# FFN gate and up projections as seven block products in two token passes

## The chip, the cores and the metric

The kernel runs on one core of a Trainium2 chip. What counts is device time in microseconds from one launch to its end, as the median of several runs. The engines are TensorE (PE; its weight loads PEld are listed apart), VectorE (DVE), ScalarE (ACT), GpSimd (POOL) and SyncE (SP), which here only issues DMAs. Each engine works through its own queue in order and waits on semaphores for the others.

## What is computed

One step of a two-layer backbone on 1280 tokens (1024 latent, then 256 context) of width 1024. Layer 0 mixes by neighbourhood attention and a state-space scan, layer 1 by a Fourier transform. Each layer ends with an FFN whose width D_FF is 2816 = 22 x 128. Cut to the FFN:

```python
def _swiglu(h, wg, wu, wd):
    return (jax.nn.silu(h @ wg) * (h @ wu)) @ wd
# in each layer, with shift, scale and gate from the conditioning:
# h = rmsnorm(x, g) * (1 + scale) + shift
# x = x + gate * _swiglu(h, w_gate, w_up, w_down)
```

## The kernel before

Activations lie channels on partitions, tokens along the free axis, as eight tiles xT[kt] of 128 x 1280 (the residual). Tokens go in three chunks, CH: 512, 512 and 256; the first two are latent, the third is context with its own conditioning. A product in full precision is made of three fp32r matmuls: each operand is split in a high part (a ScalarE cast) and a low part (a subtraction of the high part), and high x high, low x high and high x low are summed in PSUM (lines 104 to 111 and 99 to 102).

The function ffn (line 125) takes the 22 column blocks f of 128 one by one. G(f,c) is the gate product of chunk c, 8 x 3 matmuls of up to 512 columns, then SiLU on ScalarE; U(f,c) is the up product, after which VectorE multiplies (L142), ScalarE casts the high part (L143) and VectorE makes the low part (L144). DNp adds the down products of a pair of blocks to the residual, one PSUM bank for each output tile d and chunk, evacuated by one VectorE operation (L158). The loop alternates: gate and up of two blocks, then the 24 down sums of the pair before. Activations stay in SBUF. Weights come by SyncE DMA as 128 x 1024 tiles, wsplit (line 91) casts them on ScalarE (L95) and subtracts on GpSimd (L96).

In layer 0 the generator side = mods_v (line 922) runs beside the FFN: the conditioning vectors of layer 1, six of 1024. It loads w_mod in 128 x 512 pieces into two buffers, VectorE multiplies and adds each piece for the two conditionings (L901, L902), TensorE sums over partitions (L906). One piece is taken at each G and U. In layer 1 there is no side work.

Before the FFN the norm of each chunk is made: Rms sums squares as the residual's tiles are finished, rms_done turns them into 1/rms (TensorE sums L40, small VectorE operations, TensorE broadcast L55, a copy into R), modnorm (line 74) scales, shifts and splits into the operand tiles h. In layer 0 the attention's output projection first does chunk 0 for all d, then chunks 2 and 1; the first block's gate and up products of chunk 0 follow as soon as its norm is there. The Fourier output projection fnet_out (line 823) ends with the same sums.

The tile framework gives out buffers from pools: a tile waits until an earlier one with its tag is released. It orders each engine's instructions by the program's order where they are ready by its own estimate, so a stream may differ from the text in places.

Of the kernel before, what the change touches and what calls it, by code (L numbers as in the profile page):

```python
# [124 lines left out]
def ffn(k, wg, wu, wd, gate, h, order, side=iter(()), fin=lambda d,c: None, mid=lambda: None):  # L125
    """yields before it first reads h of a chunk, in the order given; mid(): called at points within the first block; fin(d,c): called when the residual's tile d is complete on chunk c; fin(KT,1) where its running sum is"""
    nc=k.nc; sh=[128,KT,128]
    at=k.at
    gs={}; us={}; ds={}; acts={}
    def sg(f):  # L130
        if f<NF: gs[f]=wsplit(k,wg[f],sh)
    def su(f):
        if f<NF: us[f]=wsplit(k,wu[f],sh)
    def sd(f):
        if f<NF: ds[f]=wsplit(k,wd[f].rearrange("p (k m) -> p k m",k=KT),sh,tag="dn",pool=k.dn)
    def G(f,c):
        p=proj(k,gs[f],h,c); s=at(CH[c][1])
        nc.scalar.activation(s,p,AF.Silu); return s  # L138
    def U(f,c,s,mid=lambda: None):
        p=proj(k,us[f],h,c,mid); n=CH[c][1]  # L140
        ah=at(n,F32R); al=at(n,F32R)
        nc.vector.tensor_tensor(out=s,in0=s,in1=p,op=ALU.mult)  # L142
        nc.scalar.copy(ah,s)  # L143
        nc.vector.tensor_tensor(out=al,in0=s,in1=ah,op=ALU.subtract)  # L144
        acts[f,c]=(ah,al)
# [8 lines left out]
    def DNp(fs,d,c):
        c0,n=CH[c]; p=bank(k)[:,:n]
        mm3(k,p,[(ds[f][i][:,d],acts[f,c][j]) for f in fs for i,j in ((0,0),(1,0),(0,1))])
        xs=k.xT[d][:,c0:c0+n]
        nc.vector.scalar_tensor_tensor(out=xs,in0=p,scalar=gate(d,c),in1=xs,op0=ALU.mult,op1=ALU.add)  # L158
    sg(0); su(0)
    for i,c in enumerate(order):  # L160
        yield
        g=G(0,c); mid()
        U(0,c,g,mid)
    sg(1); su(1); sd(0); sd(1); GU(1)
    for j in range(NF//2):
        fs=(2*j,2*j+1)
        if 2*j+2<NF:
            GU(2*j+2)
            for d in range(KT):
                for c in range(3): DNp(fs,d,c)  # L170
            sd(2*j+2); sd(2*j+3)
            GU(2*j+3,range(3) if 2*j+4<NF else range(2))
        else:
            for c in range(3):
# [1036 lines left out]
```

## Time and profile before

| | |
|---|---|
| three runs | 3035.39, 3030.21, 3035.36 us; median 3035.36 |
| profiled execution | span 3035.6 us, mean granted TensorE clock 0.965 |
| layer 0 | rest of the output projection and FFN: first product at 809.8, last down product at 1821.9 |
| layer 1 | FFN: first product at 2073.8, last down product at 3014.9 |

The profile is one execution. Its rows give busy times of engines, groups of instructions by line and tile, what an idle engine waited for, and the chain of work that ended last, followed back from the end. Matmul durations overlap: the pace is the distance from one start to the next, not the duration.

### The profile page before, as it was taken

Reading aid. Unit: us, or ns where it says so; the run is one execution under the profiler, and the core shown is the slowest. Engines: PE = TensorE matmul, PEld = TensorE weight load, DVE = VectorE, ACT = ScalarE, POOL = GpSimd, SP = SyncE. Lnnn points to the kernel's source line nnn. Section 1 sums busy time; section 2 is a strip of 40 time slices with the busy share of each in tenths; the row PEclk is TensorE's granted clock in tenths of the full one; section 3 lists DMA queues with packets and bytes.
Section 4 is the critical chain, followed back from the end, with each engine's and each line's share of the span. In section 5 each row is a group of like instructions: output and inputs, shape, how many; then the busy total and the mean of one; then the engine's idle time right before and its main releaser. Section 6 shows DMA issues by size and latency. Waiting matters only on the chain. (4 is left out here: it accounts for less than half of the span.)

```text
span 3035.6 us, 40128 instructions
## 1 busy us (share of the span) xinstructions
PE 2818.0 (93%) x15982; PEld 2338.7 (77%) x15982; DVE 1589.5 (52%) x2710; ACT 802.9 (26%) x1512; POOL 963.0 (32%) x709
## 2 busy tenths in 40 slices
PE   3778889888999999999999997998999999999997
PEld 1556667677788888888888886886888888888885
DVE  8788823888465445545554248276332223332335
ACT  3333344666342111111111123244111111111113
POOL 3666636454432111111111135264111111111114
PEclk7889999999999999999999998998999999999998
DMA  6244465354303222222212112421111111111101
GB/s 223 79 117 131 139 165 167 107 126 142 108 28 104 71 69 63 73 67 70 84 56 63 42 63 79 139 70 35 32 38 42 42 35 42 35 37 41 36 28 70
DMA packets 158563, 239.81 MB, mean 79 GB/s; under 512 B 22300, under 2 KB 97692, under 8 KB 158376
## 3 DMA queue, kind: packets, MB, share of 16 engines
q1 hardware_dynamic: 155784, 232.52, 25.2%
q0 software_dynamic: 2592, 4.73, 0.5%
q8 instruction: 125, 2.05, 0.3%
q14 instruction: 62, 0.51, 0.1%
HBM read 209.52 MB, written 27.69 MB: 78 GB/s over the span
## 5 line engine op out<-in xcount | busy, mean ns | idle before, releaser
L110 PE MATMUL p<-h,wh 128*128 128x512 f32 (+1 forms) x4480 | 1201.3, 356 | 10.4 <-DVE h L85 5.8
L110 PEld LDWEIGHTS p<-h,wh 128*128 128x128 f32 x4480 | 790.8, 189 | 145.4 <-DVE h L85 8.1
L96 POOL TENSOR_TENSOR wl<-raw,wh 128x1024 fp32r<-128x1024 f32 (+1 forms) x200 | 425.2, 2132 | 1498.6 <-ACT wh L95 1495.6
L110 PE MATMUL p<-h,wl 128*128 128x512 f32 (+1 forms) x2240 | 794.8, 355 | 0.5 <-POOL wl L96 0.5
L102 PE MATMUL p<-a,wh 128*128 128x512 f32 (+1 forms) x2112 | 572.9, 357 | 1.6 <-ACT a L143 1.6
L110 PEld LDWEIGHTS p<-h,wl 128*128 128x128 f32 x2240 | 423.5, 189 | 66.1 <-POOL wl L96 1.1
L142 DVE TENSOR_TENSOR a<-a,p 128x512 f32<-128x512 f32 x132 | 78.8, 597 | 681.4 <-PE p L110 681.4
L158 DVE SCALAR_TENSOR_TENSOR xt<-p,mod,xt 128x512 f32<-128x512 f32 (+1 forms) x528 | 336.2, 659 | 174.5 <-PE p L102 173.9
L102 PEld LDWEIGHTS p<-a,wh 128*128 128x128 f32 x2112 | 374.3, 188 | 67.3 <-ACT a L143 1.9
L102 PE MATMUL p<-a,wl 128*128 128x512 f32 (+1 forms) x1056 | 376.8, 357 | 0.0
L95 ACT CAST wh<-raw 128x1024 fp32r<-128x1024 f32 (+1 forms) x200 | 181.6, 919 | 688.3 <-PE p L102 370.9
L102 PEld LDWEIGHTS p<-a,wl 128*128 128x128 f32 x1056 | 198.6, 188 | 32.2 <-issue 0.5
L143 ACT CAST a<-a 128x512 fp32r<-128x512 f32 x132 | 72.3, 548 | 555.6 <-DVE a L142 411.1
L122 PE MATMUL p<-h,wh 128*128 128x512 f32 (+1 forms) x576 | 181.7, 385 | 19.4 <-ACT h L71 11.9
L144 DVE TENSOR_TENSOR a<-a 128x512 fp32r<-128x512 f32 (+1 forms) x132 | 146.0, 1107 | 65.2 <-ACT a L143 64.4
L138 ACT ACTIVATE a<-p 128x512 f32<-128x512 f32 x132 | 69.2, 524 | 373.0 <-PE p L110 360.9
L122 PEld LDWEIGHTS p<-h,wh 128*128 128x128 f32 x576 | 107.1, 196 | 51.6 <-ACT h L71 13.4
L902 DVE SCALAR_TENSOR_TENSOR ma<-mw,sc,ma 128x512 f32<-128x512 f32 x84 | 101.8, 1212 | 57.7 <-DMA mw<-in_w_mod_dram 57.2
L122 PE MATMUL p<-h,wl 128*128 128x512 f32 (+1 forms) x288 | 106.1, 369 | 0.0
L544 POOL TENSOR_TENSOR P<-P,l 128x384 f32<-128x384 f32 (+1 forms) x80 | 68.0, 852 | 105.7 <-DVE l L541 67.9
L550 ACT ACTIVATE P<-P,m 128x896 f32<-128x896 f32 x64 | 66.7, 1042 | 32.5 <-DVE m L549 32.3
L548 DVE CUSTOM_DVE_ANT_0 P<-S,bt 128x896 f32<-128x896 f32 x64 | 69.2, 1082 | 11.1 <-DMA bt<-T_dr 5.3
(372 smaller groups left out, 3526.3 us busy)
## 6 DMA issues: line engine op xcount, KB each, us to landing
mw<-in_w_mod_dram SPq DMA_DIRECT2D x160, 256.0 KB
raw<-in_wg_dram SPq DMA_DIRECT2D x44, 512.0 KB
raw<-in_wu_dram SPq DMA_DIRECT2D x44, 512.0 KB
raw<-in_wd_dram SPq DMA_DIRECT2D x44, 512.0 KB
xt<-in_x_dram SPq DMA_DIRECT2D x16, 640.0 KB
hf<-in_w_mod_dram SPq DMA_DIRECT2D x16, 512.0 KB
raw<-in_w_in_dram SPq DMA_DIRECT2D x24, 256.0 KB
raw<-q_dr SPq DMA_DIRECT2D x16, 320.0 KB
```

Source lines behind the costliest of these rows:

```text
L95: nc.scalar.copy(h,raw)
L96: nc.gpsimd.tensor_tensor(out=l,in0=raw,in1=h,op=ALU.subtract)
L102: k.nc.tensor.matmul(p,lhsT=w,rhs=x,start=i==0,stop=i==n-1)
L110: k.nc.tensor.matmul(p,lhsT=w[i][:,kt],rhs=h[c][j][:,kt],start=kt==0 and m==0,stop=kt==KT-1 and m==2)
L122: k.nc.tensor.matmul(ps[c],lhsT=w[i][:,kt],rhs=h[c][j][:,4*pc+kt],start=pc==0 and kt==0 and m==0,stop=pc==1 and kt==3 and m==2)
L138: nc.scalar.activation(s,p,AF.Silu); return s
L142: nc.vector.tensor_tensor(out=s,in0=s,in1=p,op=ALU.mult)
L143: nc.scalar.copy(ah,s)
L144: nc.vector.tensor_tensor(out=al,in0=s,in1=ah,op=ALU.subtract)
L158: nc.vector.scalar_tensor_tensor(out=xs,in0=p,scalar=gate(d,c),in1=xs,op0=ALU.mult,op1=ALU.add)
L548: V.tensor_tensor_reduce(out=P,in0=S,in1=b,op0=ALU.add,op1=ALU.max,scale=1.0,scalar=-3.0e38,accum_out=m)
L902: else: V.scalar_tensor_tensor(out=acc[s],in0=w,scalar=sc,in1=acc[s],op0=ALU.mult,op1=ALU.add)
```

## The change

The two projections of the FFN become block products after Strassen (Winograd's form). The 1024 input channels are halved (channel tiles 0 to 3 and 4 to 7), the 2816 columns are halved (block f goes with block f + 11), and a pass of 640 tokens is halved into 320 and 320. A 2 x 2 block product then takes seven products of 4 x 3 matmuls on 320 columns instead of eight. There are two passes over the tokens, 11 units each, 22 units in a layer, and 14 steps in a unit (STEP: gate or up X, product P). All of gate and up comes first; the activations go to DRAM (act) and come back for the down products, which are a second phase with the same matmuls as before.

Weight side: prep() makes the sums and differences of the four weight blocks on VectorE, wslot() splits each (cast on ScalarE, low part on GpSimd for products 1, 2, 4 and on VectorE for 6, 5, 7, 3); five steps are prepared ahead. Token side: early() makes the first two operands of the first pass in layer 0, full() the whole first pass, stage() the second pass's operands in units 3 to 6, which are parked in DRAM (hop), and fetch() brings them back and splits them in unit 10. Product side: step() gathers the products in three PSUM banks for each of gate and up, with ScalarE reading the first of each and VectorE adding; at the end VectorE multiplies gate by up. mods_v is now taken once after each step, in pieces of 128 x 256 (four quarters of eight loads and one closing piece for each vector). The down phase has one generator for its loads, casts and splits.

fnet_out takes its scratch from the new pool E and sums squares in two halves of 640 tokens. In layer 0 the norm of chunk 0 is finished and the old pool closed before the rest of the output projection. Comments and docstrings are gone everywhere. The core of the diff:

```diff
-def ffn(k, wg, wu, wd, gate, h, order, side=iter(()), fin=lambda d,c: None, mid=lambda: None):
...
-    def GU(f,cs=range(3)):
-        ss={}
-        for c in cs: ss[c]=G(f,c); next(side,None)
-        sg(f+1)
-        for c in cs:
-            U(f,c,ss[c])
-            next(side,None)
-        su(f+1)
-    def DNp(fs,d,c):
-        c0,n=CH[c]; p=bank(k)[:,:n]
-        mm3(k,p,[(ds[f][i][:,d],acts[f,c][j]) for f in fs for i,j in ((0,0),(1,0),(0,1))])
...
+PAIRS=NF//2; HALF=320
+STEP=((0,1),(1,1),(0,2),(1,2),(0,6),(1,6),(0,5),(0,7),(1,5),(1,7),(0,4),(0,3),(1,4),(1,3))
+SLOT={1:0,2:1,6:2,5:3,7:4,4:5,3:6}
...
+def wslot(k, src, eng):
+    w=k.E.tile([128,2,4,128],F32R,tag="w",bufs=7,name="w")
+    k.nc.scalar.copy(w[:,0],src); eng.tensor_tensor(out=w[:,1],in0=src,in1=w[:,0],op=ALU.subtract)
+    return w
+def rawt(k, src):
+    t=k.E.tile([128,8,128],F32,tag="raw",bufs=6,name="raw"); k.nc.sync.dma_start(t,src); return t
...
+    AHEAD=5
+        self.seq=[(u,X,P) for u in range(2*PAIRS) for X,P in STEP]
...
+    def early(self):
+        k=self.k; nc=k.nc; self.first=True
+        for kt in range(KT):
+            t=k.at(HALF); s=kt//4; self.scaled(t,kt,0,HALF)
+            hi=self.ops.hi(s)[:,kt%4]; self.shifted(hi,t,kt,0,HALF)
+            nc.vector.scalar_tensor_tensor(out=self.ops.lo(s)[:,kt%4],in0=t,scalar=self.S(kt,0),in1=hi,op0=ALU.add,op1=ALU.subtract)
...
+    def full(self):
+        k=self.k; V=k.nc.vector; G=k.nc.gpsimd; h=[]
+        def tt(o,i,j,op): V.tensor_tensor(out=o,in0=i,in1=j,op=op)
+        for kt in range(KT):
+            t=k.at(2*HALF); h.append(t); self.scaled(t,kt,0,2*HALF); self.shifted(t,t,kt,0,2*HALF)
+            if not self.first: self.split(kt//4,kt%4,t[:,0:HALF],G if kt%2 else V)
+        L=slice(0,HALF); N=slice(HALF,2*HALF)
+        for i in range(4):
+            a,b=h[i],h[i+4]
+            self.split(6,i,b[:,N],G)
+            tt(a[:,L],a[:,N],a[:,L],ALU.subtract)
+            tt(a[:,N],b[:,N],a[:,N],ALU.subtract)
+            tt(b[:,N],b[:,N],a[:,L],ALU.subtract)
+            self.split(2,i,b[:,N])
+        for i in range(4): self.split(3,i,h[i][:,L])
+        for i in range(4): self.split(4,i,h[i][:,N],G)
+        for i in range(4):
+            tt(h[i+4][:,L],h[i+4][:,L],h[i+4][:,N],ALU.subtract); self.split(5,i,h[i+4][:,L])
+    def stage(self, i):
+        k=self.k; nc=k.nc; V=nc.vector; t0=2*HALF; L=slice(0,HALF); N=slice(HALF,2*HALF)
+        def tt(o,x,y): V.tensor_tensor(out=o,in0=x,in1=y,op=ALU.subtract)
+        def put(s,t): nc.sync.dma_start(self.hop[s][:,HALF*i:HALF*i+HALF],t)
+        a,b,c,d=[k.at(2*HALF) for _ in range(4)]
+        for t,kt in ((a,i),(b,i+4)): self.scaled(t,kt,t0,2*HALF); self.shifted(t,t,kt,t0,2*HALF)
+        put(0,a[:,L]); put(1,b[:,L]); put(6,b[:,N])
+        tt(c[:,L],a[:,N],a[:,L]); tt(c[:,N],b[:,N],a[:,N]); put(3,c[:,L]); put(4,c[:,N])
+        tt(d[:,L],b[:,N],c[:,L]); tt(d[:,N],b[:,L],d[:,L]); put(2,d[:,L]); put(5,d[:,N])
+    def fetch(self, s):
+        nc=self.k.nc; hi,lo=self.ops.hi(s),self.ops.lo(s); r=lo.bitcast(F32)
+        nc.sync.dma_start(r,self.hop[s].rearrange("p (k n) -> p k n",k=4))
+        nc.scalar.copy(hi,r); (nc.gpsimd if s in (1,5) else nc.vector).tensor_tensor(out=lo,in0=r,in1=hi,op=ALU.subtract)
+    def load(self, u, half):
+        if u<2*PAIRS:
+            for X in range(2): self.raw[u,X,half]=rawt(self.k,self.w[X][u%PAIRS+PAIRS*half])
+    def prep(self):
+        if self.np==len(self.seq): return
+        i=self.np; self.np+=1; u,X,P=self.seq[i]; k=self.k; V=k.nc.vector
+        def tt(o,x,y,op=ALU.subtract): V.tensor_tensor(out=o,in0=x,in1=y,op=op)
+        r1=self.raw[u,X,0]; a11,a12=r1[:,0:4],r1[:,4:8]
+        if P not in (1,2): r2=self.raw[u,X,1]; a21,a22=r2[:,0:4],r2[:,4:8]
+        if P==6:
+            s3=self.st[X]=k.E.tile([128,4,128],F32,tag="st",bufs=2,name="st")
+            tt(s3,a11,a21); tt(a21,a21,a22,ALU.add); tt(a11,a21,a11)
+        if P==3: tt(a12,a12,a11)
+        src=a11 if P in (1,6) else a12 if P in (2,3) else a21 if P==5 else a22 if P==4 else self.st[X]
+        self.ws[i]=wslot(k,src,k.nc.gpsimd if P in (1,2,4) else V)
+    def start(self):
+        for _ in range(self.AHEAD): self.prep()
+    def step(self, i):
+        k=self.k; nc=k.nc; V=nc.vector; u,X,P=self.seq[i]; e=self.es
+        if P==1:
+            for b in "ABC": e[X,b]=bank(k)[:,0:HALF]
+            e[X,1]=k.at(2*HALF)
+        if P==7: e[X,2]=k.at(2*HALF)
+        p=e[X,"A" if P in (1,6,7,4) else "B" if P==2 else "C"]; w=self.ws.pop(i); x=(self.ops.hi(SLOT[P]),self.ops.lo(SLOT[P]))
+        n=0
+        for kt in range(4):
+            for a,b in ((0,0),(1,0),(0,1)):
+                nc.tensor.matmul(p,lhsT=w[:,a,kt],rhs=x[b][:,kt],start=P in (1,2,5) and n==0,stop=n==11,skip_group_check=P!=2); n+=1
+        L=slice(0,HALF); N=slice(HALF,2*HALF); e1,e2=e[X,1],e.get((X,2))
+        def done(o):
+            if X==0: nc.scalar.activation(o,o,AF.Silu)
+        def add(o): V.tensor_tensor(out=o,in0=p if P!=7 else e[X,"C"],in1=o,op=ALU.add); done(o)
+        def mul(b,s):
+            g=e[0,b][:,s]; V.tensor_tensor(out=g,in0=g,in1=e[1,b][:,s],op=ALU.mult)
+        if P==1: nc.scalar.copy(e1[:,L],p)
+        elif P==2: add(e1[:,L])
+        elif P==6: nc.scalar.copy(e1[:,N],p)
+        elif P==7: nc.scalar.copy(e2[:,N],p); add(e2[:,N])
+        elif P==4:
+            if X==0: nc.scalar.activation(e2[:,L],p,AF.Silu)
+            else:
+                g=e[0,2]; V.tensor_tensor(out=g[:,L],in0=g[:,L],in1=p,op=ALU.mult)
+                mul(2,N); self.out(u,1,g)
+        elif P==3:
+            add(e1[:,N])
+            if X==1: mul(1,L); mul(1,N); self.out(u,0,e[0,1])
+    def out(self, u, half, t):
+        p,f=divmod(u,PAIRS); self.k.nc.sync.dma_start(self.act[f+PAIRS*half][:,2*HALF*p:2*HALF*p+2*HALF],t)
+    def run(self, fin=lambda d,c: None):
+        last=PAIRS-1; self.dprep()
+        for i,(u,X,P) in enumerate(self.seq):
+            s=i%len(STEP)
+            if s==2: self.load(u+1,0)
+            if s==12: self.load(u+1,1)
+            self.prep(); self.step(i); next(self.side,None)
+            if u in (3,4,5,6) and s==5: self.stage(u-3)
+            if u==last and X==1: self.fetch(SLOT[P])
+            if u==2*PAIRS-1 and s in (6,9,11,13): next(self.dn)
+        for _ in self.side: pass
+        self.down(fin)
...
+            for j in range(PAIRS):
+                fs=(2*j,2*j+1); raws=[rawt(k,self.wd[f].rearrange("p (k m) -> p k m",k=KT)) for f in fs]
+                for i,f in enumerate(fs):
+                    t=k.H.tile([128,3840],F32,tag=f"h{f%4}",name="ac"); self.ac[f]=t
+                    nc.sync.dma_start(t[:,0:NT],self.act[f])
+                yield
+                for i,f in enumerate(fs):
+                    t=self.ac[f]; hi=t[:,NT:2*NT].bitcast(F32R); lo=t[:,2*NT:3*NT].bitcast(F32R)
+                    nc.scalar.copy(hi,t[:,0:NT]); (nc.gpsimd if i else nc.vector).tensor_tensor(out=lo,in0=t[:,0:NT],in1=hi,op=ALU.subtract)
+                    self.ac[f]=(hi,lo)
+                yield
+                for dh in range(2):
+                    for i,f in enumerate(fs): self.ds[f,dh]=wslot(k,raws[i][:,4*dh:4*dh+4],nc.gpsimd)
+                    yield
+        self.dn=gen()
...
+        for j in range(PAIRS-1):
+                if d in (0,2,4,6): next(self.dn,None)
+                for c in range(3): one((2*j,2*j+1),d,c)
+        for c in range(3):
+            if c==2: fin(KT,1)
+            for d in range(KT): one((NF-2,NF-1),d,c); fin(d,c)
...
+def mods_v(k, us):
+    a,b=k.at(512),k.at(512); n=[0]
+    def mw(): n[0]+=1; return a[:,256*(n[0]%2):256*(n[0]%2)+256]
+    for u in us: yield from mod_unit_v(k,u,mw,[b[:,256*i:256*i+256] for i in range(2)])
...
+    act=dr("act",[NF,128,NT]); hop=dr("hop",[7,128,4*HALF])
...
+        wout(d,0,p); r0.add(d)
+    r0.done(Rt[0])
+    arp.__exit__(None,None,None); Ep=epool()
...
+    F=FFN(k,*ffw(0),mv(0,5),mv(0,4),mv(0,3),Rall,act,hop)
...
+        if d==2: F.early()
...
+    F.load(0,0); F.load(0,1); F.start()
+    r[1].done(Rt[1]); r[2].done(Rt[2])
+    F.full(); F.side=mods_v(k,[(1,j) for j in range(6)])
+    F.run(fin)
...
+    F=FFN(k,*ffw(1),mv(1,5),mv(1,4),mv(1,3),Rall,act,hop)
+    r=fnet_out(k,io,mv(1,2),*AB,lambda: (F.load(0,0),F.load(0,1)))
+    F.start()
+    F.full(); F.run(fin2)
```

The helpers that it calls: scaled() is one VectorE operation (residual times scale times R) on each stretch of latent or context tokens, shifted() one ScalarE operation that adds the shift, split() a ScalarE cast and a subtraction on the engine given, Ops the table of the 14 operand pieces in the six tiles that held h. In mod_unit_v the loop runs over quarters of 256 columns instead of halves of 512.

## Rows read from the trace of the kernel before

**Rows 1.** The page: span, then busy us (share of the span) xinstructions.

```profile
span 3035.6 us, 40128 instructions
...
PE 2818.0 (93%) x15982; PEld 2338.7 (77%) x15982; DVE 1589.5 (52%) x2710; ACT 802.9 (26%) x1512; POOL 963.0 (32%) x709
```

**Rows 2.** Stretches: length, busy us of PE, PEld, DVE, ACT, POOL; clock, DMA, GB/s.

```profile
973.00:1640.00 667.00, 667.00 (x3520) 563.08 (x3519) 335.22 (x471) 100.66 (x154) 116.48 (x48) 1.00 0.24 72
...
2060.00:2115.00 55.00, 43.80 (x186) 33.39 (x187) 42.23 (x73) 28.84 (x52) 24.61 (x17) 0.84 0.04 10
...
2250.00:2950.00 700.00, 700.00 (x3615) 592.10 (x3614) 229.42 (x314) 99.80 (x148) 117.14 (x49) 1.00 0.12 37
```

**Rows 3.** Chain in order of time, layer 1's FFN: start, us, what.

```profile
2111.62 56.12 PE p L110 x287
2167.74 27.85 PE p L102 x144
2195.59 56.08 PE p L110 x288
...
2531.36 55.69 PE p L110 x288
```

**Rows 4.** Timeline of PE in the Fourier output projection.

```profile
1998.78 1.63 PE L845 MATMUL O<-h,wpm 128*128 128x320 f32 x10
...
2002.85 2.06 PE L840 MATMUL E<-h,wpm 128*128 128x322 f32 x12
...
2005.57 3.78 PE L845 MATMUL O<-h,wpm 128*128 128x320 f32 x24
```

**Rows 5.** A DVE group by shape: busy us, mean ns, idle before.

```profile
L818 DVE TENSOR_TENSOR a<-raw 128x512 f32<-128x512 f32 x7 | 4.8, 680 | 3.0 <-DMA raw<-in_Wb_dram 3.0
```

**Rows 6.** The chain at the Fourier projection's end and layer 1's FFN start.

```profile
2024.83 0.60 DVE a L818
2025.43 0.60 DVE a L30
...
2061.02 4.42 PE ms L40 x20
...
2068.09 4.62 PE rb L55 x6
...
2096.82 0.67 DVE a L79 x2
2097.49 0.40 DVE a L83
...
2098.60 12.26 PE p L110 x76
```

**Rows 7.** Lines 142 and 158: duration ns min/median/max.

```profile
L142 DVE TENSOR_TENSOR a<-a,p x132: 404/686/690, 895.7 to 3008.8; 128x512 f32<-128x512 f32 x88, 128x256 f32<-128x256 f32 x44
...
L158 DVE SCALAR_TENSOR_TENSOR xt<-p,mod,xt x528: 467/746/753, 978.1 to 3017.3; 128x512 f32<-128x512 f32 x172, 128x256 f32<-128x256 f32 x4
```

**Rows 8.** Line 96: duration ns min/median/max, first and last start.

```profile
L96 POOL TENSOR_TENSOR wl<-raw,wh x200: 1251/2399/2887, 58.6 to 2953.3; 128x1024 fp32r<-128x1024 f32 x69, 128x512 fp32r<-128x512 f32 x31
```

**Rows 9.** ACT groups by shape.

```profile
L95 ACT CAST wh<-raw 128x512 fp32r<-128x512 f32 x60 | 37.0, 618 | 102.8 <-PE p L122 41.2 <-PE p L1024 20.2 <-PE p L1097 17.9
...
L848 ACT ACTIVATE a<-O,mod 128x320 f32<-128x320 f32 x8 | 4.2, 529 | 1.2 <-PE O L845 1.2
```

**Rows 10.** Timeline of DVE and POOL, two stretches.

```profile
2025.96 0.68 DVE L818 TENSOR_TENSOR raw<-raw 128x512 f32<-128x512 f32 x1
...
2026.17 2.56 POOL L820 TENSOR_TENSOR wpm<-a,wpm 128x512 fp32r<-128x512 f32 x1 [2.83 <-ACT wpm L820]
...
2504.41 2.39 POOL L96 TENSOR_TENSOR wl<-raw,wh 128x1024 fp32r<-128x1024 f32 x1 [11.53 <-ACT wh L95]
...
2504.67 2.42 DVE L144 TENSOR_TENSOR a<-a 128x256 fp32r<-128x256 f32 x1 [0.90 <-ACT a L143]
```

**Rows 11.** The side work's DVE group and its waits.

```profile
L902 DVE SCALAR_TENSOR_TENSOR ma<-mw,sc,ma 128x512 f32<-128x512 f32 x84 | 101.8, 1212 | 57.7 <-DMA mw<-in_w_mod_dram 57.2
```

More of the change, by code (lines that the diff above doesn't have):

```diff
@@ L27, in add, with blk @@
         else: self.pend=s
+    def blk(self, j): return self.acc[1][:,128*j:128*j+128]
     def flush(self):
@@ L39, in rms_done @@
     for i,(r,j) in enumerate(cols):
-        nc.tensor.matmul(ms[:,0:m],lhsT=r.acc[1][:,128*j:128*j+128],rhs=k.ecol[:,9-i:9-i+m],start=i==0,stop=i==m-1)
+        nc.tensor.matmul(ms[:,0:m],lhsT=r.blk(j),rhs=k.ecol[:,9-i:9-i+m],start=i==0,stop=i==m-1)
     if split: yield
@@ L123, in proj3 @@
     return ps
-def ffn(k, wg, wu, wd, gate, h, order, side=iter(()), fin=lambda d,c: None, mid=lambda: None):
[L127 to L145, printed above, removed]
-    def GU(f,cs=range(3)):
-        ss={}
-        for c in cs: ss[c]=G(f,c); next(side,None)
-        sg(f+1)
-        for c in cs:
-            U(f,c,ss[c])
-            next(side,None)
-        su(f+1)
-    def DNp(fs,d,c):
-        c0,n=CH[c]; p=bank(k)[:,:n]
-        mm3(k,p,[(ds[f][i][:,d],acts[f,c][j]) for f in fs for i,j in ((0,0),(1,0),(0,1))])
[L157 to L168, printed above, removed]
-            for d in range(KT):
[L170 to L174, printed above, removed]
-                if c==2: g=G(NF-1,2); fin(KT,1); U(NF-1,2,g)
-                for d in range(KT): DNp(fs,d,c); fin(d,c)
@@ new lines, with __init__, part, hi @@
+PAIRS=NF//2; HALF=320
+STEP=((0,1),(1,1),(0,2),(1,2),(0,6),(1,6),(0,5),(0,7),(1,5),(1,7),(0,4),(0,3),(1,4),(1,3))
+SLOT={1:0,2:1,6:2,5:3,7:4,4:5,3:6}
+class Ops:
+    def __init__(self, k):
+        self.k=k; self.h={}
+    def part(self, i):
+        t,o=(i//3,1280*(i%3)) if i<12 else (i-8,0)
+        if t not in self.h: self.h[t]=self.k.H.tile([128,3840 if t<4 else 1280],F32R,tag=f"h{t}",name=f"op{t}")
+        return self.h[t][:,o:o+1280].rearrange("p (k n) -> p k n",k=4)
+    def hi(self, s): return self.part(2*s)
+    def lo(self, s): return self.part(2*s+1)
@@ L827, in ld, with square @@
     def ld(d):
-        raw=k.ar.tile([128,8,128],F32,tag="raw",bufs=2,name="raw"); h,l=[k.dn.tile([128,8,128],F32R,tag="dn",bufs=4,name="wpm") for _ in range(2)]
+        raw=k.E.tile([128,8,128],F32,tag="raw",bufs=6,name="raw"); h,l=[k.E.tile([128,8,128],F32R,tag="w",bufs=7,name="wpm") for _ in range(2)]
         s=lambda t: [t[:,0:4],t[:,4:8]]
         return wpm(k,io,d,s(raw),a(512).rearrange("p (g c) -> p g c",g=4),s(h),s(l))
-    rms=[Rms(k,c,k.at,True) for c in range(3)]
+    acc=[None,None]
+    def square(d):
+        for i in range(2):
+            s=a(640); nc.scalar.activation(s,k.xT[d][:,640*i:640*i+640],AF.Square)
+            if acc[i] is None: acc[i]=s
+            else: (V if i else nc.gpsimd).tensor_tensor(out=acc[i],in0=acc[i],in1=s,op=ALU.add)
     Wn=lambda d: k.R[d//4][0:4,128*(d%4):128*(d%4)+128]
@@ L859, in fnet_out @@
         upd(1024,0,Ea,Oa,V if d==7 else nc.gpsimd); upd(256,1024,Ep,Op,V)
-        for c in range(3): rms[c].add(d)
+        square(d)
+    rms=[Rms(k,c,None) for c in range(3)]
+    for c in range(3): rms[c].blk=lambda j,c=c: acc[(CH[c][0]//128+j)//5][:,128*((CH[c][0]//128+j)%5):][:,0:128]
     return rms
@@ L920, in mod_gain @@
         k.nc.vector.scalar_tensor_tensor(out=o,in0=o,scalar=1.0,in1=g.to_broadcast([128,g.shape[1],2]),op0=ALU.add,op1=ALU.mult)
-def mods_v(k, us, pool):
-    for u in us: yield from mod_unit_v(k,u,pool)
+def mods_v(k, us):
+    a,b=k.at(512),k.at(512); n=[0]
+    def mw(): n[0]+=1; return a[:,256*(n[0]%2):256*(n[0]%2)+256]
+    for u in us: yield from mod_unit_v(k,u,mw,[b[:,256*i:256*i+256] for i in range(2)])
 def mods(k, us, pool, bufs, width=1024):
@@ L1097, in build @@
                     nc.tensor.matmul(p,lhsT=w[x][:,kt],rhs=o[0][y][:,4*pc+kt],start=pc==0 and kt==0 and i==0,stop=pc==1 and kt==3 and i==2)
-        wout(d,0,p); r.add(d)
-    arp.__exit__(None,None,None); right()
-    md=mods_v(k,[(1,j) for j in range(6)],k.dn)
+        wout(d,0,p); r0.add(d)
+    r0.done(Rt[0])
+    arp.__exit__(None,None,None); Ep=epool()
     def lring():
```

109 lines of the change are left out of this document (56 added, 53 removed).

## The prediction

> **What bounds the kernel now.** I read the page's busy times first [rows 1]: TensorE is busy in 93% of the span, VectorE in 52%, GpSimd in 32%. Then the stretches [rows 2]: in the two FFN stages TensorE is busy in all of 667 and 700 us at full clock, while VectorE has 335 and 229 us of work. VectorE's load differs because the first FFN (layer 0) carries the conditioning sums for layer 1 beside it and the second does not. The chain [rows 3] runs from one block of gate and up products to the next block of down products with nothing between. So today the FFN is TensorE's alone, and each layer spends 11 x 56.0 = 616 us on gate and up and 11 x 28.0 = 308 us on down. The question is whether TensorE stays the bound when its work shrinks and everybody else's grows.
>
> **TensorE's part.** Seven products replace eight. A unit (128+128 columns of F, 640 tokens, gate and up) is 14 steps of 12 matmuls on 320 columns. The odd half of the Fourier output projection already runs this form [rows 4]: ten in 1.63 us, the last lasting 0.31, so 1.32/9 = 147 ns from start to start; the group of 24 gives (3.78 - 0.31)/23 = 151. I take 147: 1.76 us a step, 24.7 us a unit, 22 units = 543 us a layer, 73 less than 616. At 151 it would be 558 and 58 less. The down products keep their matmuls and their shapes.
> The Trainium skill ("TensorE: Matmul & The Clock Gate", Back-to-back issue gap) has N/2.4 + 2.5 ns, 135.8 ns for 320 columns, by which a layer would take 502 us and both together 82 us less than my sum, some 2965. For the blocks of [rows 3] the same rule gives 192 x 215.8 + 96 x 109.2 ns = 51.9 us where they took 55.7 to 56.1, so the trace does not agree and its pace stands.
>
> **VectorE and GpSimd, a unit without side work.** Prices first. A 128x512 operation with two SBUF inputs lasts 0.68 us [rows 5], and one follows the next after 0.60; on 256 columns after 0.34 (two in 0.67) [rows 6]; 320 columns, in between, 0.40. With one PSUM input it lasts 0.69 on 512 and 0.40 on 256 columns [rows 7], less the same 0.08 of overlap: 0.40 for 320. GpSimd's shortest 512 split is 1.25 us [rows 8].
> Added to VectorE: for each of gate and up, four sums of weight blocks and four low parts (blocks 6, 5, 7, 3): 16 x 0.60 = 9.6 us. From step(): three adds for each and one product from PSUM, 7 x 0.40 = 2.8, and three products in SBUF, 1.2. Together 13.6 us. GpSimd takes the low parts of blocks 1, 2, 4: 6 x 1.25 = 7.5 us. ScalarE takes 14 casts of 0.62 and ten PSUM reads of about 0.5 [rows 9]: 14 us, not the bound.
>
> **The disputed price: do the two engines' times add?** Look at [rows 10]. GpSimd's 2.39 us split starts at 2504.41, and a 256-column subtraction on VectorE, 0.4 us by itself, starts 0.26 us later and takes 2.42. It ends 0.29 us after GpSimd does: it waited. In the other stretch VectorE runs on and a GpSimd split of 512 takes 2.56 instead of 1.25. Operations with a PSUM input never show this (L142 at most 0.690, L158 at most 0.753, in 660 of them [rows 7]). So two-input SBUF work on VectorE and work on GpSimd take turns. A unit then needs 9.6 + 1.2 + 7.5 = 18.3 us of turns, and with VectorE's PSUM work 21.1 if none of that falls beside GpSimd: under 24.7 either way. Layer 1's FFN stays TensorE's.
> The Trainium skill says the same ("SBUF — State Buffer", Who interferes with whom: VectorE with two SBUF inputs and a GpSimd instruction that reads SBUF exclude each other for a whole instruction). It speaks against this change, which loads both at once; by it the next sum stands near 31 us, without it VectorE alone needs 23.6 and hides.
>
> **Layer 0, with side work.** mods_v has 6 vectors x 4 quarters x 9 pieces = 216 pieces, one after each step, so it lasts 216/14 = 15.4 of the 22 units. 192 pieces hold two operations on 256 columns at 0.40 (a single one: [rows 6]): 10.0 us a unit. Turns: 18.3 + 10.0 = 28.3 us; with the PSUM work 31.1. Both are over 24.7, so for 15.4 units these two engines set the pace. Between 28.3 and 31.1 I take 31: GpSimd holds its turn for 7.5 us in 31, and only a PSUM operation that comes just then is hidden. 15.4 x 31 = 477. In the same stretch stage() comes four times (four scalings on 384 and 256 columns, 1.8 us, and six differences, 2.4: 17 us in all), and in unit 10 the seven fetches split 1280 columns each: VectorE five at 1.5, by length, and GpSimd two, at least 2.4 (its median, mostly 1024 columns [rows 8]), taken as 2.9: 13. So +30. The remaining 6.6 units at 24.7: 163. Layer 0: 670 us, 54 more than 616. From below, at 28.3, it is 628, +12.
> Layer 1: 543. Its units have 24.7 - 21.1 = 3.6 us to spare, which cover stage() (4.2 us each time) but for 0.6 x 4 and leave of the fetches' 13 us some 9, less what five steps of weights prepared ahead bridge (8.8 us): I put 5 on both, between 0 and 11. Low parts that come late now and then: between 0 and 1.5 us a unit, I take 0.3, near the lower end, since 3.6 is spare: 7. Layer 1: 555, 61 less.
>
> **The start and the hand-over.** Before, from the end of the Fourier projection to the norm's broadcast is 2061.0 to 2072.7, and products run without a pause only from 2098.6 [rows 6]. The new start needs the same sums and broadcasts, then full(): eight scalings of 640 columns (0.60 x 640/512 = 0.75) and 14 more operations before the third block product has its first operands, about 8 us, beside four steps (7 us) that are ready in layer 0 through early(). In layer 0 r0.done() and the new pool now stand between the two parts of the output projection: its sums, a broadcast of 4 to 5 us for all three chunks [rows 6], a load and a split of the first weights: from 0 if the pool's space is free, to 13 us. I take 10 for layer 0 and 2 for layer 1: 12. The down phase loads 2.3 MB for each 28 us, with weights in six slots and activations in two pairs of tiles, one pair ahead: hidden; the first pair can start only behind unit 21's third product, and I put 3 us a layer on it (0 to 10): 6. If that cover goes, TensorE waits for its splits at each pair.
>
> **The sum.** The profiled execution lasted 3035.6 us; the median of the runs is 3035.36, so the two count as one. +54 - 61 + 12 + 6 = +11: **3047 us**.
>
> **Rivals.**
> 1. *Faster: the side work hides.* If the order of the instructions lets the PSUM operations and every wait fall into GpSimd's turns, units cost 28.3 in layer 0 (-42 against my sum), and with starts at nothing (-12) and no late parts (-7) that gives 2986. If turns cost nothing at all, units are 25.5 (0.8 for waits): 393 + 163 + 10 = 566, and 2943. My sum crosses 3029 at 29.8 us a unit; below 28.6 (3010) it is this rival's. For it: VectorE alone has 13.6 + 10.0 = 23.6, under 24.7. Against: [rows 10].
> 2. *Slower still: waits on top of the turns.* Each weight sum goes VectorE, ScalarE, VectorE (0.62 in the middle [rows 9]); mods_v has two half tiles for its loads, and VectorE waited 57.7 us for such loads already [rows 11]; its TensorE sums come behind VectorE. At 34 us a unit (+46), 1.5 us more a unit in layer 1 (+33) and starts of 27 (+15): 3141.
> 3. *The change doesn't do what it says:* the narrow matmuls do not keep 147 ns when accumulators switch twelve by twelve. The neighbouring 322-column group shows 2.06 us for 12, (2.06 - 0.31)/11 = 159 ns [rows 4]: 26.7 us a unit, +44 in layer 1 and +13 in layer 0's last units: 3104.
>
> **How the numbers follow.** Mine 0.50, with a range of its own of 3010 to 3090 (28.6 to 33.8 us a unit); rival 1 0.30; rival 2 0.15; rival 3 0.05. About 0.2% (6 us) is what a measurement of this kernel can tell. Of my 0.50, 0.12 lies below 3029, 0.08 between 3029 and 3042, 0.30 above. Rival 1 is faster, 2 and 3 slower: faster 0.42, same 0.08, slower 0.50. The range leaves out a tenth on each side: 2955, near the foot of rival 1, to 3130, near rival 2.
>
> **What the profile after would show.** Right: matmuls of 320 columns 147 ns apart in both layers; in layer 0's first 15 units TensorE busy about 80% and VectorE over 90%, many two-input operations lasting 1.2 us or more, units of some 31 us; then, as mods_v ends, units of 25 us; layer 1 at 25 us throughout; the down pairs still 28 us. Wrong if layer 0 shows no step between its units with and without side work (rival 1), if TensorE waits in layer 1 as well (rival 2), or if it is busy throughout and yet slow (rival 3). A granted clock below 1.00 in layer 0's first units, which the kernel before shows only where TensorE pauses (0.84 [rows 2]), would add to rival 2.

## The result, and the profile after

The changed kernel takes 3103.97 us (median; 3099.28 to 3108.0) where the kernel before takes 3034.73 beside it: a ratio of 1.023, interval 1.0216 to 1.0245. It is slower by 69 us; forecast were 11. The profiled execution of the changed kernel has a span of 3106.2 us, 70.6 more than before's [rows 1]. Its page, the rows that answer to [rows 1]:

```profile
span 3106.2 us, 46852 instructions
...
PE 2771.2 (89%) x17062; PEld 2445.4 (79%) x17062; DVE 2229.8 (72%) x3928; ACT 1182.1 (38%) x2356; POOL 1212.3 (39%) x951
```

TensorE is busy 47 us less and the span is 71 us longer. Where, the stretches tell (columns as in [rows 2]; in order: layer 0's first unit, its units 2 to 15, its last units, its down phase, layer 1's first unit, its other units, its down phase):

```profile
907.50:955.20 47.70, 35.32 (x177) 32.41 (x176) 44.17 (x73) 26.56 (x54) 16.27 (x14) 0.75 0.23 72
955.20:1438.30 483.10, 419.47 (x2486) 385.53 (x2486) 439.00 (x794) 188.77 (x381) 136.85 (x86) 0.90 0.46 148
1438.30:1612.40 174.10, 174.10 (x1184) 172.84 (x1183) 122.21 (x186) 85.96 (x172) 60.09 (x42) 1.00 0.38 125
1612.40:1932.00 319.60, 313.48 (x1605) 266.13 (x1603) 193.68 (x308) 59.81 (x82) 102.13 (x66) 0.98 0.24 83
2194.00:2233.90 39.90, 31.88 (x169) 30.43 (x170) 35.95 (x54) 24.45 (x54) 24.30 (x18) 0.80 0.15 53
2233.90:2764.60 530.70, 522.56 (x3530) 519.48 (x3529) 396.74 (x582) 266.21 (x532) 188.92 (x128) 0.99 0.39 131
2764.60:3088.00 323.40, 314.86 (x1606) 267.89 (x1604) 197.79 (x312) 68.76 (x96) 111.64 (x73) 0.98 0.21 75
```

Read the second row against the third. Where side work runs, 14 units take 483.1 us (34.5 each), TensorE stands for 64 us and VectorE is busy 91%; when the side work has ended, units take 24.6 to 25.9 and TensorE never stands. The matmuls on 320 columns start 147 ns apart (median of all 7392), as forecast. [Rows 2] had TensorE busy in all of its FFN stretches at clock 1.00; now three stretches show 0.75 to 0.90.

The difference of the two spans by parts, each cut at the first or last matmul of its kind. In the kernel before, gate and up (616 us in a layer, as the prediction reads it) and down alternate; three of the 22 blocks, 84 us, come before the first down product and 532 us behind it, and its parts are counted by these.

| part | forecast | measured | off by |
|---|---|---|---|
| layer 0 gate and up: first unit | 31 us | 47.7 | +16.7 |
| units 2 to 15, with stage and fetch | 464 | 483.1 | +19.1 |
| the rest of it | 175 | 174.1 | -0.9 |
| layer 1 gate and up: first unit | 24.7 | 39.9 | +15.2 |
| the rest of it | 530.3 | 530.7 | +0.4 |
| before the first units, both layers | +12 against before | +18.3 | +6.3 |
| down phases, both layers | +6 against before | +11.1 | +5.1 |
| all else, behind the last down product | 0 | -2.3 | -2.3 |
| sum | +11 | +70.6 | +59.6 |

So gate and up give -45.4 in layer 1 (570.6 for 616) and cost +88.9 in layer 0 (704.9 for 616). Of the 18.3 us before the first units, 17.9 lie in layer 0.

What held layer 0's units 2 to 15 shows in three views. VectorE and GpSimd by lines there (busy us, mean ns, idle before, as in [rows 5]):

```profile
L1035 DVE SCALAR_TENSOR_TENSOR e<-e,sc 128x256 f32<-128x256 f32 x313 | 182.7, 626 | 4.0 <-DMA e<-in_w_mod_dram 3.5 <-DVE e L1035 0.3
L216 DVE TENSOR_TENSOR raw<-raw 128x512 f32<-128x512 f32 x86 | 68.9, 805 | 1.3 <-POOL w L144 1.2
...
L241 DVE TENSOR_TENSOR e<-p,e 128x320 f32<-128x320 f32 x84 | 40.6, 483 | 8.3 <-PE p L237 5.9 <-ACT e L247 2.2
L216 DVE TENSOR_TENSOR st<-raw 128x512 f32<-128x512 f32 x28 | 26.5, 948 | 3.9 <-DMA raw<-in_wg_dram 3.9
...
L144 POOL TENSOR_TENSOR w<-raw,w 128x512 fp32r<-128x512 f32 x84 | 130.7, 1567 | 331.4 <-ACT w L144 268.2 <-DVE e L241 23.2 <-DMA e<-in_w_mod_dram 14.5
```

Two-input operations that read SBUF alone last 805 and 948 ns where [rows 5] has 680, and GpSimd's splits 1567 where its shortest is 1251 [rows 8]; L241, with one PSUM input, lasts 0.48 here and in experiment 1, where GpSimd has no splits of weights. Then TensorE's waits and VectorE's in the same stretch (line waited for, us, times, longest):

```profile
PE p L1038 <- DVE e L1035: 54.6, 20, 4.8
PE p L237 <- DVE e L241: 4.9, 3, 2.9
...
DVE mod L1044 <- PE p L1042: 14.6, 14, 1.7
DVE w L144 <- ACT w L144: 6.4, 9, 2.1
```

TensorE stands 54.6 us before the sums of the side work (L1038) and only 8.5 before block products. The next block matmuls start only behind such a sum: one starts at 991.08 after 3.28 us of standing, and the next block matmul at 992.37. VectorE in turn stands 14.6 us until the transposes of the same sums are done (L1042), of 44.1 us in which it is idle (483.1 less 439.0).

### The profile page after: what moved, and what is told of

It reads as the page before. It is cut to its first block, busy times and chain, and to the rows that moved or that the text cites. A ratio compares the mean times of both kernels' runs of the same rounds, so it can differ in the third digit from the quotient of the medians.

```text
span 3106.2 us, 46852 instructions
## 1 busy us (share of the span) xinstructions
PE 2771.2 (89%) x17062; PEld 2445.4 (79%) x17062; DVE 2229.8 (72%) x3928; ACT 1182.1 (38%) x2356; POOL 1212.3 (39%) x951
## 5 line engine op out<-in xcount | busy, mean ns | idle before, releaser
L237 PE MATMUL p<-op,w 128*128 128x320 f32 x7392 | 1151.3, 317 | 36.8 <-DVE e L241 12.9
L237 PEld LDWEIGHTS p<-op,w 128*128 128x128 f32 x7392 | 1127.5, 194 | 63.4 <-issue 16.7
L144 POOL TENSOR_TENSOR w<-raw,w 128x512 fp32r<-128x512 f32 x368 | 524.7, 1441 | 1145.2 <-ACT w L144 1031.0
L103 PE MATMUL p<-ac,w 128*128 128x512 f32 (+1 forms) x3168 | 618.9, 358 | 0.0
L103 PEld LDWEIGHTS p<-ac,w 128*128 128x128 f32 x3168 | 527.5, 191 | 90.5 <-issue 2.1
L144 ACT CAST w<-raw 128x512 fp32r<-128x512 f32 x632 | 380.3, 619 | 510.7 <-issue 228.9
L216 DVE TENSOR_TENSOR raw<-raw 128x512 f32<-128x512 f32 x264 | 233.6, 896 | 50.1 <-POOL w L144 45.6
L144 DVE TENSOR_TENSOR w<-raw,w 128x512 fp32r<-128x512 f32 x264 | 188.1, 715 | 47.7 <-ACT w L144 45.4
L1035 DVE SCALAR_TENSOR_TENSOR e<-e,sc 128x256 f32<-128x256 f32 x336 | 197.8, 631 | 4.0 <-DMA e<-in_w_mod_dram 3.5
L123 PE MATMUL p<-h,wh 128*128 128x512 f32 (+1 forms) x576 | 182.0, 386 | 18.0 <-ACT h L72 11.5
L241 DVE TENSOR_TENSOR e<-p,e 128x320 f32<-128x320 f32 x264 | 127.6, 483 | 29.0 <-PE p L237 13.4
L123 PEld LDWEIGHTS p<-h,wh 128*128 128x128 f32 x576 | 107.1, 196 | 50.4 <-ACT h L72 12.4
L216 DVE TENSOR_TENSOR st<-raw 128x512 f32<-128x512 f32 x88 | 84.5, 960 | 72.8 <-DMA raw<-in_wg_dram 62.0
L97 POOL TENSOR_TENSOR wl<-raw,wh 128x512 fp32r<-128x512 f32 x60 | 88.3, 1474 | 80.8 <-ACT wh L96 78.4
L123 PE MATMUL p<-h,wl 128*128 128x512 f32 (+1 forms) x288 | 106.5, 370 | 0.0
L283 POOL TENSOR_TENSOR ac<-ac 128x1280 fp32r<-128x1280 f32 x22 | 65.3, 2968 | 80.3 <-ACT ac L283 76.8
L1038 PE MATMUL p<-e,one 128*32 128x256 f32 x96 | 27.9, 482 | 58.1 <-DVE e L1035 57.8
```

Source lines behind the costliest of these rows:

```text
L97: nc.gpsimd.tensor_tensor(out=l,in0=raw,in1=h,op=ALU.subtract)
L103: k.nc.tensor.matmul(p,lhsT=w,rhs=x,start=i==0,stop=i==n-1)
L123: k.nc.tensor.matmul(ps[c],lhsT=w[i][:,kt],rhs=h[c][j][:,4*pc+kt],start=pc==0 and kt==0 and m==0,stop=pc==1 and kt==3 and m==2)
L144: k.nc.scalar.copy(w[:,0],src); eng.tensor_tensor(out=w[:,1],in0=src,in1=w[:,0],op=ALU.subtract)
L216: def tt(o,x,y,op=ALU.subtract): V.tensor_tensor(out=o,in0=x,in1=y,op=op)
L237: nc.tensor.matmul(p,lhsT=w[:,a,kt],rhs=x[b][:,kt],start=P in (1,2,5) and n==0,stop=n==11,skip_group_check=P!=2); n+=1
```

## The experiments

All are edits of the changed kernel; ratios are to the kernel before, run on the same chip.

**1. No turns: every low part of a weight on VectorE.**

```diff
-        self.ws[i]=wslot(k,src,k.nc.gpsimd if P in (1,2,4) else V)
+        self.ws[i]=wslot(k,src,V)
```

> All low parts of the weight operands are made on VectorE, none on GpSimd (both layers). Turns theory (VectorE's two-input SBUF work and GpSimd's work exclude each other): a unit with side work loses 7.5 us of GpSimd turns and gains 6 x 0.60 = 3.6 us on VectorE, so the 14 units from the second to the fifteenth of layer 0 go from 34.5 to about 30.5 us each and the whole to about 3050 us; layer 1's units stay at 24.7, as VectorE has 17.2 us there. Rival, VectorE's own load and its waits are the price and GpSimd costs it nothing: units 34.5 + 3.6 = 38 us, the whole about 3155 us.

3034.23 us, ratio 1.0007 (0.9998 to 1.0016): 70 us gained by giving VectorE more work. Layer 0's gate and up 649.5, layer 1's 557.9. VectorE by lines and the stretch of units 2 to 15:

```profile
L1035 DVE SCALAR_TENSOR_TENSOR e<-e,sc 128x256 f32<-128x256 f32 x308 | 141.0, 493 | 11.0 <-DMA e<-in_w_mod_dram 10.7
L144 DVE TENSOR_TENSOR w<-raw,w 128x512 fp32r<-128x512 f32 x168 | 112.0, 683 | 4.7 <-ACT w L144 4.6
L216 DVE TENSOR_TENSOR raw<-raw 128x512 f32<-128x512 f32 x84 | 57.3, 682 | 0.0
...
L216 DVE TENSOR_TENSOR st<-raw 128x512 f32<-128x512 f32 x28 | 19.1, 682 | 0.0
```
```profile
944.20:1378.30 434.10, 396.87 (x2487) 364.41 (x2486) 408.61 (x870) 184.96 (x380) 7.15 (x2) 0.98 0.51 164
```

It beat the 3050 us expected: layer 1, which was to stay, fell by 12.7 us, and layer 0's first unit by 7.5 (47.7 to 40.2). Each form is back at its own length (805 and 948 to 682, 626 to 493), and VectorE's busy time falls from 439.0 to 408.6 although it took over 84 splits. The unit prices hold: 14 x (13.6 + 3.6 + 10.0) = 381, and 25 of stage and fetch, is 406 (402 with the four differences that stage() makes, L198 x16 in four calls, where the prediction counted six). The turns are real, and dear.

**2. The side work spread**: a piece after every third step, the others in the down phase.

```diff
-            self.prep(); self.step(i); next(self.side,None)
+            self.prep(); self.step(i)
+            if i%3==0: next(self.side,None)
...
+        self.down(fin)
         for _ in self.side: pass
-        self.down(fin)
...
+                for _ in range(2 if d%3==0 else 1): next(self.side,None)
                 for c in range(3): one((2*j,2*j+1),d,c)
```

> A piece of the conditioning sums after every third step only; the other 113 pieces run beside the down sums. Turns theory: a unit has 21.1 + 14/3 x 0.8 = 24.8 us of VectorE and GpSimd work, TensorE 24.7, so units of 25 to 26 us in layer 0; gate and up of layer 0 go from 705 to about 580 us, the down phase of layer 0 grows by 0 to 15, the whole is 2975 to 2995 us, below both kernels. Rival, the loss of layer 0 lies in its start, its pool change and its hand-over: the whole stays above 3060 us.

3020.09 us, ratio 0.9953 (0.9937 to 0.9969): 0.5% faster than before, less than expected. Layer 0's gate and up fell by 93 us (704.9 to 611.9) while its down phase rose by 15 (TensorE's busy time there from 313.5 to 328.6, with 12.7 us of the sums that moved). But units 2 to 21 still take 27.1 us, not 25. VectorE's and TensorE's waits in them:

```profile
DVE st L216 <- DMA raw<-in_wg_dram: 33.0, 18, 3.0
DVE raw L216 <- POOL w L144: 15.8, 9, 1.8
...
PE p L237 <- DVE e L241: 24.4, 21, 3.4
```

**3. Without TensorE's part of the side work.**

```diff
-        p=bank(k,tag="m")
-        for s in range(2): nc.tensor.matmul(p[32*s:32*s+32,0:256],lhsT=k.one1,rhs=ma[s],start=True,stop=True)
...
         yield
-        t=bank(k,tag="m")
...
-        mod_gain(k,u,o,c)
```
(the conditioning of layer 1, which these would have made, is a constant here)

> Leaves out the sums over partitions of the side work on TensorE and what follows from them (the conditioning vectors of layer 1 are set to a constant); VectorE's 384 operations stay. Turns theory: VectorE and GpSimd set the pace, TensorE's wait for the side sums is only the place where their lag shows; it will show elsewhere and the units stay at 31 to 34 us, the whole at 3070 to 3104 us. Rival, TensorE's 20 waits for these sums (54.6 us) and the lower clock after them are the price: units of 25 to 28 us, the whole below 3030 us.

3053.34 us, ratio 1.0067 (1.0052 to 1.0082): neither theory. The stretch of units 2 to 15:

```profile
942.00:1385.80 443.80, 379.01 (x2354) 366.77 (x2353) 434.03 (x763) 177.59 (x361) 137.13 (x86) 0.94 0.50 161
```

It takes 443.8 us, 39 less, with VectorE busy 434.0 of them (98%). So the turns alone, with next to no waiting for TensorE (VectorE 0.7 us), are 31.7 us a unit, of which 2 are stage and fetch; the other 2.8 of the 34.5 came with the sums. That could be their work (25.8 + 9.0 us of TensorE) or the wait for them; experiment 7 parts these.

**4. A second profile of the spread version.**

> The same kernel as the spread one, a second look for the spread between executions of its units: within 0.3% of it by either theory.

3022.74 us in a single run, in line with experiment 2, and no more is drawn from it.

**5. Both edits, 1 and 2.** Here and in experiments 6, 9 and 11 the side work of the down phase stands behind an output tile's products, in experiment 2 before them.

> Both edits: every low part of a weight on VectorE, and a piece of side work after every third step, the rest in the down phase. Turns theory: no GpSimd work is left in a unit, VectorE has 13.6 + 3.6 + 3.3 = 20.5 us a unit, so TensorE sets layer 0 too: units near 25.2 where the spread alone had 27.1, which is 37 us, and the 13 us that the low parts on VectorE gave in layer 1: 3020 - 37 - 13 = 2970. Rival: the gains do not add, because what held the spread version's units at 27.1 is VectorE's wait for the second half of the raw weights (36 us in layer 0) and not the turns: then only layer 1 gains, 3007.

2968.23 us, ratio 0.9786 (0.9772 to 0.9801): what the turns theory gave (2970), and 65 us faster than before. Stretches: layer 0's first unit, its units 2 to 21, its down phase; layer 1's first unit and the rest.

```profile
900.70:939.00 38.30, 28.87 (x171) 27.51 (x170) 36.17 (x67) 25.39 (x51) 7.83 (x8) 0.87 0.25 81
939.00:1444.90 505.90, 505.41 (x3421) 496.26 (x3421) 454.96 (x867) 260.54 (x515) 6.36 (x2) 1.00 0.44 150
1470.80:1805.70 334.90, 328.90 (x1684) 271.87 (x1682) 291.83 (x521) 65.90 (x97) 104.55 (x64) 0.98 0.35 117
2066.40:2105.50 39.10, 30.59 (x169) 28.83 (x170) 35.06 (x61) 25.01 (x55) 15.29 (x12) 0.83 0.15 56
2105.50:2624.60 519.10, 517.67 (x3529) 517.40 (x3529) 409.03 (x703) 271.63 (x530) 13.27 (x7) 1.00 0.39 134
```

TensorE is the bound again in both layers, at clock 1.00, but for the first units. VectorE is busy 90% of layer 0's stretch and hides.

**6. Experiment 2 with an earlier load**, for the wait of 33 us that it showed.

```diff
-            if s==12: self.load(u+1,1)
+            if s==9: self.load(u+1,1)
```

> The spread version with the load of a unit's lower weight blocks issued after step 9 and not after step 12. If VectorE's 36 us of waiting for these loads in layer 0, and TensorE's 24 us of waiting for VectorE's adds that follow from it, are what keeps the units at 27.1: units near 25.8 and 2990 to 3000. Rival, the turns keep them there: 3018 to 3022, the load's wait gone and VectorE's operations longer.

3014.61 us, ratio 0.9942 (0.9927 to 0.9957): not to be told from experiment 2. The waits hardly moved (30.6 us for the gate weights, 21.8 of TensorE for L241), so the place of the load in the program was not what delayed it. In experiment 5 the same wait is 4.6 us with the load where it was. So GpSimd's splits stood behind it. SyncE's own waits show one way: before the raw loads it stands 80.0 us in experiment 2 until GpSimd's splits have read the raw tile, and 78.4 us with the earlier load (window 947 to 1480 of both). In experiment 5 it stands 105.4 us there for VectorE's splits instead, and the loads still come in time; how much of the delay is the tile, and how much SyncE's queue, where stores wait too, is not parted.

**7. The side sums later, nothing taken away.** A second pair of accumulators; sums, transposes and addition in three stages.

```diff
+    b=[k.at(512),k.E.tile([128,512],F32,tag="acc",bufs=1,name="acc")]
...
+            ma=[b[q%2][:,256*s:256*s+256] for s in range(2)]
...
+                if kt in (2,4,6): next(old,None)
...
+            old=mod_sums(k,u,q,ma)
```

> The changed kernel with a second pair of accumulators for the side work, so that TensorE's sums of a quarter come two steps into the next quarter, its transposes two steps later and VectorE's addition of them two steps after that. Nothing is taken away. If TensorE's wait in its own queue for the side sums (54.6 us) and VectorE's wait for the transposes (14.6 us) are what came on top of the turns: near 3060, a little over the 3053 without these sums. Rival, the turns hold everything back and the wait only moves to the next instruction: 3090 or more.

3063.92 us, ratio 1.0103 (1.0088 to 1.0118), 40 less than the change and as expected. The stretch of units 2 to 15 and TensorE's waits in it (L1029 are the sums):

```profile
949.50:1397.20 447.70, 403.86 (x2484) 372.81 (x2483) 434.10 (x784) 185.47 (x379) 134.15 (x86) 0.94 0.48 158
```
```profile
PE p L1029 <- DVE e L1059: 17.4, 7, 4.3
PE p L1029 <- DVE acc L1059: 13.8, 8, 4.0
```

The same work in 447.7 us and not 483.1, near the 443.8 without the sums: the coupling was dear, not TensorE's work. TensorE still waits 31 us, but VectorE hardly waits for it: it is idle 13.6 us of the stretch, where the change had 44.1.

**8. The first units: the operands' low parts on VectorE.**

```diff
-            self.split(6,i,b[:,N],G)
+            self.split(6,i,b[:,N])
...
-        for i in range(4): self.split(4,i,h[i][:,N],G)
+        for i in range(4): self.split(4,i,h[i][:,N])
```
(and the odd tiles of the first two operands in layer 1)

> The changed kernel with the low parts of the first pass's operands (8 in layer 0, 12 in layer 1) on VectorE and not on GpSimd, in the start of each gate and up phase only. In that start VectorE is busy 36 of 40 us and GpSimd 24. If the turns make the first unit long (47.7 and 39.9 us), it becomes 5 to 9 us shorter in each layer: 3087 to 3094. Rival, the start is bound by VectorE's own work and the order of the operands: 3104 or more.

3094.63 us, ratio 1.0198 (1.0181 to 1.0215). The first units of the two layers:

```profile
900.50:947.80 47.30, 36.01 (x177) 31.70 (x175) 38.72 (x77) 26.40 (x54) 15.54 (x6) 0.79 0.22 73
2183.90:2220.40 36.50, 30.44 (x168) 28.45 (x169) 34.53 (x65) 24.64 (x54) 15.65 (x6) 0.86 0.17 58
```

They are 47.3 and 36.5 us (47.7 and 39.9), so these splits were a small part. That does not rule the turns out: GpSimd is still busy 15.5 and 15.7 us with splits of weights. Other runs part them. Without the weight splits on GpSimd the first units are 40.2 and 38.9 us (experiment 1), with the side work spread 40.7 and 39.4 (experiment 2), and with no GpSimd work and no side work in them 36.6 and 36.9 (experiment 9), of which VectorE is busy 32.6 and 33.5.

**9. All early edits together**: 1 and 8, with side work after three steps of seven from the second unit on.

> Low parts of the weights and of the first pass's operands all on VectorE, the side work after three steps of every seven from the second unit on, the rest in the down phase. No GpSimd work is left in a gate and up phase but two fetches. From the version with both edits (2968): the first unit of layer 0 loses its five pieces of side work (3 us of VectorE) and the turns of the operands' low parts (the changed kernel gained 3 and 4 us of it in its two layers): near 2960. Rival, the first units are bound by VectorE's own 35 us there and gain nothing: 2968 or more.

2969.6 us, ratio 0.9789 (0.9773 to 0.9805): no better than experiment 5. That is the number of the rival, but not its mechanism: the first units did fall, from 38.3 and 39.1 us to 36.6 and 36.9. Layer 0's other units, where the side work is denser, took 538.0 us for 531.8, the fetch's unit 29.9 for 26.9. (Experiment 8 had gained 0.4 and 3.4 us in the first units, not the 3 and 4 that the expectation names.)

**10. Edits 1 and 7**, side work after each step as in the change.

> The changed kernel with both the low parts of the weights on VectorE and the side sums on TensorE later, side work after each step as in the change. VectorE then has 13.6 + 3.6 + 10.0 us a unit and 2.1 for stage and fetch: 29.3, against 31.0 measured with the low parts on VectorE alone. If the rest of that (14 units of 1.7, 25 us) was TensorE's and VectorE's waiting for each other over the side sums: 14 units of 29.3 and a total near 3010. Rival, it was the wait for ScalarE's copies and for loads: 3030 or more.

3028.26 us, ratio 0.9977 (0.9965 to 0.9988): 6 less than experiment 1, near the rival. Units 2 to 15 take 425.9 us, 30.4 each. VectorE is busy 405.0 us of these (95%), so the sums have little left to cost. Of the other 20.9 us it stands 11.6 before loads of the side work and 4.0 for ScalarE's casts; TensorE waits 15.9 us for ScalarE's casts of the weights. That is the rival's mechanism.

**11. Cover for the norm in the last down pair**, on experiment 5.

```diff
-                for c in range(3): one((2*j,2*j+1),d,c)
+                for c in range(2 if j==PAIRS-2 and d>3 else 3): one((2*j,2*j+1),d,c)
...
-            if c==2: fin(KT,1)
+            if c==2:
+                for d in range(4,8): one((NF-4,NF-3),d,2)
+                fin(KT,1)
...
-        for i in {(3,1): (0,),(KT,1): (0,1),(3,2): (1,)}.get((d,c),()):
+        for i in {(3,1): (0,),(KT,1): (0,1),(6,2): (1,)}.get((d,c),()):
```

> The version with both edits (2968), and in each down phase the last chunk's products of the last pair but one, for four of the eight output tiles (24 matmuls on 256 columns, some 2.7 us), held back until just before the norm's broadcast of the last pair, and the second chunk's broadcast three output tiles later. Nothing is added. If TensorE's waits for the norm's sums and broadcasts there (4.3 us in layer 0, 7.6 in layer 1) stand because the change took the gate and up block out from between, they go for the most part: 2958 to 2963. Rival, the norm's chain ends at the same time and TensorE waits behind the next instruction: 2966 or more.

2965.64 us, ratio 0.9774 (0.976 to 0.9787), not to be told from experiment 5. In layer 0 the down phase fell from 335.0 to 329.5 us and the wait for the broadcast from 3.0 to 1.7. In layer 1 it stayed (320.7 to 320.1): one wait for a broadcast is 7.8 us now, where VectorE also has the output's scaling to do. Half right.

## Why the prediction was right and wrong

- **TensorE's pace: right.** 147 ns a matmul, 24.7 us a unit; layer 1's units after the first took 530.7 us for a forecast of 530.3. Rival 3 is out, and that its 3104 us are the time measured is chance. The estimate of 135.8 ns for 320 columns by the formula of the Trainium skill ("TensorE: Matmul & The Clock Gate", Back-to-back issue gap) isn't seen here. The section calls that formula one for a single matmul; its 131 ns for 512 columns in a stream aren't seen either, as the 512-column down products start 229 ns apart (median).
- **The turns: right, in kind and about in size.** Experiments 3 and 7 show 31.7 and 32.0 us a unit for a forecast of 33.1 (31, and stage and fetch over 14 units). Experiment 1 shows that it is GpSimd's presence and not VectorE's load. The Trainium skill states that VectorE with two SBUF inputs and GpSimd reading SBUF exclude each other ("SBUF — State Buffer", Who interferes with whom), and the trace agrees: 948 ns beside GpSimd's splits, 682 without.
- **The step that failed most is the start.** The prediction put 12 us on it ("I take 10 for layer 0 and 2 for layer 1: 12"), with about 8 us until the third block product has operands, and took the first units like any other, as 31 and 24.7 us. Before the first units it was 18.3 us, and these measured 47.7 and 39.9: 38 of the 60 us by which the sum was off. For full() goes on behind the third product: by the prediction's prices VectorE has 8 x 0.75 + 16 x 0.40 + 12 x 0.40 = 17.2 us there, beside the unit's own 13.6, and TensorE meets one unfinished operand after the other. Experiment 9 leaves 12 us over 24.7 in each layer with neither GpSimd nor side work in the first unit. The rest, 11 us in layer 0 and 3 in layer 1, went with these two, and 6.3 of the 11 were in the forecast of 31. That VectorE's work sets the 12 us is argued from its busy time, not tried. In layer 0 the pause before the second part of the output projection, forecast at up to 13, is 16 us. TensorE's last product starts at 811.37, the next at 827.28, after a load into the new pool that SyncE issues only behind the norm's broadcast, having stood 24.0 us for it:

```profile
811.37 0.39 PE L1224 MATMUL p<-h,wh 128*128 128x512 f32 x1
...
821.19 0.58 ACT L57 COPY R<-rb 128x512 f32<-128x512 f32 x1 [7.98 <-PE rb L56]
821.28 8.89 SPq L148 DMA_DIRECT2D raw<-in_w_out_dram  x7
826.62 2.33 ACT L144 CAST w<-raw 128x512 fp32r<-128x512 f32 x4 [4.84 <-DMA raw<-in_w_out_dram]
...
827.28 0.80 PE L103 MATMUL p<-h,w 128*128 128x512 f32 x1 [6.13 <-ACT w L144]
```

- **The step that failed in layer 0's units** is "Between 28.3 and 31.1 I take 31": it priced the turns and left the waits between TensorE and VectorE over the side sums at nothing, in rival 2 alone ("its TensorE sums come behind VectorE"). They are 2.5 us a unit, 35 us in 14 units (483.1 to 447.7, experiment 7). It is luck that the stretch came out only 19 over: the turns had been put 1.1 us a unit too high.
- **The down phase: the right worry, the wrong place.** The first pair starts at once (the next matmul starts 0.15 us behind the last product's start), and ten pairs take 27.7 us each. The last pair cost 16 us, 42.2 and 45.8 where the kernel before takes 34.8 and 36.8 besides its gate and up; the ten pairs gave 6 back (277.3 us in each layer for 281.3 and 279.7). There the kernel before runs matmuls of its last gate and up block between the norm's sums and its broadcast (24 of them from 2995.6 to 2998.7 us); the change takes them away, and the prediction didn't name them as cover. TensorE's waits in layer 1's down phase:

```profile
PE rb L56 <- DVE e L55: 7.2, 2, 4.2
PE ms L41 <- POOL e L31: 1.3, 1, 1.3
```

  The kernel before has only the second of these, 1.3 us, up to its last product, and one of 1.6 us for ScalarE. By its profile experiment 11 gained 5.5 us in layer 0 with such cover.
- **The sign** came out as the likeliest case had it. The time lies inside the whole range, but 14 us above that case's own (3010 to 3090), between the case (3047) and rival 2 (3141): turns, with waits on top, and starts of 50 us where rival 2 had 27. Rival 1 is out for this kernel, yet its time is what experiment 5 reaches once the GpSimd splits are gone and the side work is spread: 2968 lies between its 2943 and 2986.
- **What stays open:** by which way GpSimd's splits delay the raw weights' loads in experiment 2, what sets the 12 us that the first units keep in experiment 9, and what the lower clock cost by itself.

## What to carry to other kernels

When a scheme trades matmuls for elementwise sums, price the sums as turns: in this kernel splits handed from VectorE to GpSimd came back as longer VectorE operations, and taking them back gave 70 us. Count all the work that prepares the operands of a new phase, not only what its first products need; here that was the largest miss. Look in each engine's stream for instructions of side work whose operand comes from the engine that is now full: issue them some steps later, with a second accumulator, or spread the side work to where its engines have time. And when a block is removed or moved, ask what it covered; here that was a norm's chain of small steps.
